# Beside a layer's last head: each output tile is projected as soon as its columns are transposed

## The chip, the cores and the metric

The kernel runs on one core of one Trainium2 chip. The metric is the device time of one execution in microseconds (us), lower is better. The kernel before takes 1910.28 us, the median of three runs that lie between 1908.68 and 1917.12 us. Five engines work side by side, each through its own instructions in order: PE (TensorE, matrix products and transposes), DVE (VectorE), ACT (ScalarE), POOL (GpSimd) and SP, which here only issues transfers. They wait for each other by semaphores.

## The reference, cut to what matters

Four layers run one after another over 640 tokens (128 of the prompt, 512 of the sample), that is five tiles of 128 tokens. A layer normalises x, projects it into eight heads, mixes the tokens within each head, and projects the mixed and gated heads back:

```python
for l in range(DEPTH):                       # 4 layers, kind = l % 3
    hs = rms_norm(xs, g_pre[l]) * (1.0 + sc_s) + sh_s
    if kind == 0:   ys = diff_attention(hs, da_w_in[j], da_w_out[j], ...)
    elif kind == 1: ys = retention(hs, ret_w_in[j], ret_w_out[j], ...)
    else:           ys = hgrn2(hs, hg_w_in[j], hg_w_out[j], ...)
    xs = xs + ga_s * rms_norm(ys, g_post[l])

# the end of each mixer, o is the mixed heads side by side
y = (o.reshape(B, T, HG_WIDTH) * jax.nn.silu(g)) @ w_out
```

Layers 0 and 3 are differential attention, layer 1 retention, layer 2 HGRN2. The change concerns the last line, `y @ w_out`, for the heads that are done while the last head is still being mixed.

## The kernel before

All products are in fp32 accuracy: a tensor is split into a high and a low part, and one product becomes three matmuls (high by high, high by low, low by high). For the output projection these are lines 458, 459 and 460 (`wide_unit`): one moving block of 512 columns each, over a column block k of 128 of the eight heads (16 in retention, whose heads are twice as wide). The text calls one such matmul a *product of w_out*.

Before a tile of y (128 tokens) can be projected, its columns must lie on the partitions. `y_to_h` transposes four blocks at a time on PE (line 448) into one PSUM bank; ACT copies the bank as the high part (`hh`, line 431) and DVE subtracts for the low part (`hl`, line 116). The bank is free after `hl`. PSUM is shared by two tags: "one", four buffers of one bank, and "two", two buffers of two banks.

PE's order is written out by hand; the other engines' order follows from a schedule that a list scheduler makes for that PE order. `weave(main, fill, span, room)` interleaves two generators: `main` mixes a head, `fill` projects the next head, and for every step of `main` as much of `fill` is issued as the ratio room/span allows. Beside the last head `fill` is `tail`: it transposes what is there of y (the six heads 0 to 5, in retention the eight column blocks 0 to 7, which lie in five buffers `ys` loaded from memory), takes four pieces of w_out, and then projects `hold` tiles into banks that it keeps open ("held"). `y_col` (line 497) then brings in the column of head 6 for all five tiles at once, and one product triple per held tile is added. When the last head is done `out_layer` finishes: the remaining tiles (2, 3 and 4 or only 4; tile 4 in a "two" buffer), the column of head 7, the second 512 columns and the norm.

Held tiles are 4 in layers 0 and 3, 2 in retention, 2 in HGRN2.

In HGRN2 the head's mix (`hg_mix`) runs over two directions. Each makes its decays on DVE, ACT and POOL, then transposes four blocks on PE (`pt`, line 1213), which ACT copies (`kt`), multiplies them by the values (`us`, line 1219), from which DVE makes the states `s` (line 1223) and ACT copies `so` (line 1226). Then both directions' scores (lines 1238 to 1242, into `fp`, a "two", and `gp`, a "one") are masked by DVE, and the head's output `o` (lines 1254 to 1257, a "two") is squared on ACT, scaled through `rs` on POOL, and written as y by DVE (line 637).

Of the kernel before, what the change touches and what calls it, by code (L numbers as in the profile page):

```python
# [21 lines left out]
P = 128  # L22
D = 1024
KT = 8
NS = 512
NP = 128
NT = 5
# [61 lines left out]
class Net:  # L89
# [374 lines left out]
    def tail(self, l, y, hold, st=None):  # L464

        self.mod_finish()
        two = KINDS[l] == 1
        self.held = {}
        ys = [y[:, tt, :] for tt in range(NT)]
        if two:  # L470
            for tt, (tag, bufs, dt) in enumerate((("sg", 2, F32), ("vh", 2, F32R), ("vl", 2, F32R), ("mraw", 2, F32), ("mraw", 2, F32))):
                if tag == "mraw":
                    ys[tt] = self.wp.tile([P, 4, 256], dt, tag=tag, bufs=bufs, name="ys")
                else:
                    ys[tt] = st.mp.tile([P, NT, 256], dt, tag=tag, bufs=bufs, name="ys")[:, 0:4, :]
                ys[tt] = ys[tt].rearrange("p a b -> p (a b)").bitcast(F32)
                self.nc.sync.dma_start(ys[tt], self.y_dram[:, tt, :])
        for tt in range(NT):
            yield from self.y_to_h(ys[tt], tt, KT if two else 6)
        self.ow = self.take(l, 0, 4)  # L480
        for tt in range(hold):
            ps = self.held[tt] = self.one()
            yield from self.wide_unit(ps, tt, self.ow, range(KT if two else 6), last=False)
        if not two:
            while hasattr(st, "done") and st.done < 6:
                yield None
            self.y_col(y, 6)
            yield 1.2
            for tt in range(hold):
                yield from self.wide_unit(self.held[tt], tt, self.ow, (6,), False, False)  # L490
# [559 lines left out]
    def hg(self, l, y):  # L1050
        nc, tc, t = self.nc, self.tc, self.t
        with tc.tile_pool(name=f"hg{l}", bufs=1, reuse_waits="tile") as mp:
            rs = self.const(mp, "rs")
            mf = mp.tile([P, NT, 64], U8, name="mf")
            mg = mp.tile([P, NT, 64], U8, name="mg")
            for m, n in ((mf, "mf"), (mg, "mg")):
                c = mp.tile([P, 640], F32, tag="w0", bufs=5, name="w0")[:, 0:320]
                nc.sync.dma_start(c, t["consts"][:, CWHERE[n][0]:sum(CWHERE[n])])
                nc.vector.tensor_copy(m.rearrange("p a b -> p (a b)"), c)
            ng = mp.tile([P, P], F32, name="ng")  # L1060
            nc.sync.dma_start(ng, t["hg_norm"][0].partition_broadcast(P))

            tt_ = nc.vector.tensor_tensor
            mx = mp.tile([P, 2, 8], F32, name="lmx")
            ex = mp.tile([P, 2, 4, 8], F32, name="lex")
            su = mp.tile([P, 2, 8], F32, name="lsu")
            tt_(out=mx, in0=self.lbl[:, :, 0, :], in1=self.lbl[:, :, 1, :], op=ALU.max)
            for i in (2, 3):
                tt_(out=mx, in0=mx, in1=self.lbl[:, :, i, :], op=ALU.max)
            tt_(out=ex, in0=self.lbl, in1=mx.unsqueeze(2).to_broadcast([P, 2, 4, 8]), op=ALU.subtract)  # L1070
            nc.scalar.activation(ex, ex, AF.Exp)
            tt_(out=su, in0=ex[:, :, 0, :], in1=ex[:, :, 1, :], op=ALU.add)
            for i in (2, 3):
                tt_(out=su, in0=su, in1=ex[:, :, i, :], op=ALU.add)
            nc.vector.reciprocal(su, su)
            tt_(out=ex, in0=ex, in1=su.unsqueeze(2).to_broadcast([P, 2, 4, 8]), op=ALU.mult)
            lb = mp.tile([P, 2, 8], F32, name="lb")
            tt_(out=lb, in0=ex[:, :, 0, :], in1=ex[:, :, 1, :], op=ALU.add)
            for i in range(2, l + 1):
                tt_(out=lb, in0=lb, in1=ex[:, :, i, :], op=ALU.add)  # L1080
            tt_(out=lb, in0=lb, in1=ex[:, :, 0, :], op=ALU.subtract)
            co = mp.tile([P, 3, 2, 8], F32, name="lco")
            for i, (a, b) in enumerate(((-0.5, 0.5), (0.5, 0.5), (0.5, -0.5))):
                nc.vector.tensor_scalar(out=co[:, i], in0=lb, scalar1=a, scalar2=b, op0=ALU.mult, op1=ALU.add)
            pz = [mp.tile([P, NT, 64], F32, name=f"z{d}") for d in range(2)]
            for z in pz:
                nc.vector.memset(z, 0.0)
            st = types.SimpleNamespace(mp=mp, l=l, rs=rs, mf=mf, mg=mg, ng=ng, co=co, pz=pz, iv={}, sg={}, h={})
            for _ in self.hg_proj(st, 0):
                pass  # L1090
            for h in range(HEADS):
                if h < 7:
                    self.weave(self.hg_mix(st, h, y), self.hg_proj(st, h + 1), 24.0, 30.0 if h < 6 else 18.0)
                else:
                    self.weave(self.hg_mix(st, h, y), self.tail(l, y, 2), 24.0, 12.0)

    def hg_proj(self, st, h):
        nc, t, mp = self.nc, self.t, st.mp
# [43 lines left out]
    def hg_mix(self, st, h, y):  # L1142
        nc, t, mp = self.nc, self.t, st.mp
        p, m = h // 2, h % 2
# [18 lines left out]
        for d in range(2):  # L1163
# [7 lines left out]
            if d == 0:  # L1171
                DV.tensor_tensor_scan(c, rs, g, 0.0, op0=ALU.mult, op1=ALU.add)
                ref, mid, last = 32, 63, 127
            else:
                DV.tensor_tensor_scan(c[:, ::-1], rs, g[:, ::-1], 0.0, op0=ALU.mult, op1=ALU.add)
                ref, mid, last = 31, 64, 0
# [30 lines left out]
            ke = tmp()  # L1207
            TT(PL, ke, k, ll, ALU.mult)
            yield 6.0
            pt = self.one([P, 4, P])  # L1210
            blocks = (0, 1, 2, 4) if d == 0 else (1, 2, 3, 4)
            for i, b in enumerate(blocks):
                nc.tensor.transpose(pt[:, i, :], bl(ke)[:, b, :], self.ident)
            kt = mp.tile([P, 4, P], F32, tag=f"kt{d}", name="kt")
            nc.scalar.activation(kt, pt, AF.Copy)
            yield 1.5
            us = self.one([P, 4, P])
            for i, b in enumerate(blocks):
                nc.tensor.matmul(us[:, i, :], kt[:, i, :], iv[:, b, ec], start=True, stop=True)
            order = (0, 1, 2) if d == 0 else (2, 1, 0)  # L1220
            for n, i in enumerate(order):
                b = blocks[i]
# [7 lines left out]
        (qf, kf, off, qef), (qb, kb, ofb, qeb) = res  # L1230
        fp = self.two()
        fd, fo = (fp[:, i, :320].rearrange("p (b i) -> p b i", i=64) for i in range(2))
        gp = self.one([P, NT, 64])
        mm = nc.tensor.matmul
        A, B = slice(0, 64), slice(64, 128)
        for b in range(NT):
# [196 lines left out]
```

## Time and profile before

| | |
|---|---|
| median of three runs | 1910.28 us (1908.68 to 1917.12) |
| profiled execution | 1908.83 us, span 1907.0 us |
| PE busy | 1814.8 us, 95% of the span |
| DVE / ACT / POOL busy | 1315.7 / 978.1 / 503.7 us |
| mean granted TensorE clock | 0.989 |

PE is busy for all but 92 us of the span. Busy time of a matmul is longer than its distance to the next one, since matmuls are pipelined; so the text takes distances from start to start. A granted clock of 1.00 is 2.4 GHz, 0.50 is 1.2 GHz. The last heads lie at about 380 to 405 us (layer 0), 905 to 975 (retention), 1400 to 1460 (HGRN2) and 1815 to 1845 (layer 3).

### The profile page before, as it was taken

Reading aid. Unit: us, or ns where it says so; the run is one execution under the profiler, and the core shown is the slowest. Engines: PE = TensorE matmul, PEld = TensorE weight load, DVE = VectorE, ACT = ScalarE, POOL = GpSimd, SP = SyncE. Lnnn points to the kernel's source line nnn. Section 1 sums busy time; section 2 is a strip of 40 time slices with the busy share of each in tenths; the row PEclk is TensorE's granted clock in tenths of the full one; section 3 lists DMA queues with packets and bytes.
Section 4 is the critical chain, followed back from the end, with each engine's and each line's share of the span. In section 5 each row is a group of like instructions: output and inputs, shape, how many; then the busy total and the mean of one; then the engine's idle time right before and its main releaser. Section 6 shows DMA issues by size and latency. Waiting matters only on the chain.

```text
span 1907.0 us, 32063 instructions
## 1 busy us (share of the span) xinstructions
PE 1814.8 (95%) x12060; PEld 1651.2 (87%) x12060; DVE 1315.7 (69%) x2553; ACT 978.1 (51%) x2271; POOL 503.7 (26%) x419
## 2 busy tenths in 40 slices
PE   6989999999999999999999999999979989999998
PEld 4888999977888888888878899999978879999976
DVE  5768788857788998774334667676764766667754
ACT  3456666555444344433343456666654545655552
POOL 0414343202222222222101323342431521222101
PEclk9999999999999999999999999999989999999999
DMA  9644445414345445433323222222214463443322
GB/s 323 177 114 133 133 138 144 128 57 155 126 133 168 140 143 157 142 124 101 104 99 111 85 70 73 64 62 73 62 42 138 132 172 89 112 115 88 107 72 101
DMA packets 231963, 224.59 MB, mean 118 GB/s; under 512 B 11664, under 2 KB 201984, under 8 KB 231808
## 3 DMA queue, kind: packets, MB, share of 16 engines
q1 hardware_dynamic: 231344, 222.16, 38.7%
q8 instruction: 95, 1.56, 0.4%
q14 instruction: 60, 0.49, 0.1%
q10 hardware_dynamic: 464, 0.39, 0.1%
HBM read 174.79 MB, written 18.35 MB: 101 GB/s over the span
## 4 chain that ended last, share of the span: by engine, by line
PE 57%; DVE 20%; ACT 8%; DMA 5%; issue 4%; POOL 3%; SPq 2%; DVEq 0%; ACTq 0%; POOLq 0%
PE one L458 7%; PE one L460 7%; PE one L459 7%; PE one L250 4%; PE one L251 4%; PE one L252 4%; DVE macc L361 4%; DVE wlo L116 3%; PE one L821 3%; PE one L225 3%; PE one L226 2%; PE one L227 2%; ACT whi L178 2%; DMA kz<-ks 1%; DVE nm L785 1%
## 5 line engine op out<-in xcount | busy, mean ns | idle before, releaser
L250 PE MATMUL one<-hh,whi 128*128 128x320 f32 x1152 | 365.4, 317 | 9.3 <-ACT qp L760 6.4
L251 PE MATMUL one<-hl,whi 128*128 128x320 f32 x1152 | 357.0, 310 | 0.0
L252 PE MATMUL one<-hh,wlo 128*128 128x320 f32 x1152 | 356.8, 310 | 0.0
L116 DVE TENSOR_TENSOR wlo<-raw,whi 128x1024 fp32r<-128x1024 f32 x192 | 246.4, 1290 | 134.2 <-ACT whi L178 132.9
L458 PE MATMUL one<-whi,hh 128*128 128x512 f32 x744 | 303.0, 407 | 5.8 <-ACT yo L554 2.5
L460 PE MATMUL one<-whi,hl 128*128 128x512 f32 x744 | 296.1, 398 | 1.0 <-DVE hl L116 0.5
L459 PE MATMUL one<-wlo,hh 128*128 128x512 f32 x744 | 295.6, 397 | 0.0
L178 ACT ACTIVATE whi<-raw 128x1024 fp32r<-128x1024 f32 x192 | 201.3, 1056 | 138.4 <-PE one L251 52.0
L250 PEld LDWEIGHTS one<-hh,whi 128*128 128x128 f32 x1152 | 217.6, 189 | 12.0 <-ACT qp L760 6.8
L361 DVE SCALAR_TENSOR_TENSOR macc<-mraw,smod,macc 128x256 f32<-128x256 f32 x432 | 216.3, 544 | 10.2 <-POOL macc L363 9.6
L251 PEld LDWEIGHTS one<-hl,whi 128*128 128x128 f32 x1152 | 217.6, 189 | 0.5
L252 PEld LDWEIGHTS one<-hh,wlo 128*128 128x128 f32 x1152 | 217.3, 189 | 0.3 <-DVE wlo L116 0.3
L225 PE MATMUL one<-whi,hh 128*128 128x256 f32 x720 | 207.8, 289 | 0.0
L226 PE MATMUL one<-wlo,hh 128*128 128x256 f32 x720 | 201.1, 279 | 0.0
L227 PE MATMUL one<-whi,hl 128*128 128x256 f32 x720 | 201.1, 279 | 0.0
L458 PEld LDWEIGHTS one<-whi,hh 128*128 128x128 f32 x744 | 141.3, 190 | 38.5 <-DVE p L1007 4.0
L460 PEld LDWEIGHTS one<-whi,hl 128*128 128x128 f32 x744 | 140.8, 189 | 37.1 <-DVE hl L116 2.3
L459 PEld LDWEIGHTS one<-wlo,hh 128*128 128x128 f32 x744 | 141.3, 190 | 29.4
L363 POOL TENSOR_TENSOR macc<-macc,mpart 128x512 f32<-128x512 f32 x64 | 94.7, 1481 | 180.9 <-ACT macc L359 65.3
L391 POOL TENSOR_TENSOR rs<-ms,mhalf 128x1 f32<-128x1 f32 (+1 forms) x72 | 66.0, 917 | 288.3 <-DVE ms L384 152.9
L225 PEld LDWEIGHTS one<-whi,hh 128*128 128x128 f32 x720 | 135.5, 188 | 1.5
L226 PEld LDWEIGHTS one<-wlo,hh 128*128 128x128 f32 x720 | 135.6, 188 | 0.0
(344 smaller groups left out, 3765.0 us busy)
## 6 DMA issues: line engine op xcount, KB each, us to landing
mraw<-in_w_mod SPq DMA_DIRECT2D x96, 512.0 KB, 4.2
raw<-in_da_w_in SPq DMA_DIRECT2D x56, 512.0 KB, 4.2
raw<-in_hg_w_in SPq DMA_DIRECT2D x36, 512.0 KB, 3.8
raw<-in_ret_w_in SPq DMA_DIRECT2D x64, 256.0 KB, 3.1
kk<-ks SPq DMA_DIRECT2D x64, 160.0 KB, 3.4
kz<-ks SPq DMA_DIRECT2D x64, 160.0 KB, 3.2
qq<-q SPq DMA_DIRECT2D x64, 128.0 KB, 3.5
raw<-in_da_w_out SPq DMA_DIRECT2D x16, 512.0 KB, 3.5
```

The lines of the kernel that those rows point to most:

```text
L116: return (eng or self.nc.gpsimd).tensor_tensor(out=out, in0=full, in1=hi.bitcast(F32), op=ALU.subtract)
L178: self.nc.scalar.activation(hi, raw, AF.Copy)
L225: mm(out, xh, wh[:, k % 4, :], start=(first and k == ks[0]), stop=False)
L226: mm(out, xh, wl[:, k % 4, :], start=False, stop=False)
L227: mm(out, xl, wh[:, k % 4, :], start=False, stop=(last and k == ks[-1]))
L250: nc.tensor.matmul(ps, wh[:, k, :], self.hh[:, k, c], start=(k == 0), stop=False)
L251: nc.tensor.matmul(ps, wh[:, k, :], self.hl[:, k, c], start=False, stop=False)
L252: nc.tensor.matmul(ps, wl[:, k, :], self.hh[:, k, c], start=False, stop=(k == KT - 1))
L361: nc.vector.scalar_tensor_tensor(out=m, in0=raw[:, k, :], scalar=c, in1=m, op0=ALU.mult, op1=ALU.add)
L458: mm(ps, xh, wh, start=(first and k == ks[0]), stop=False)
L459: mm(ps, xh, wl, start=False, stop=False)
L460: mm(ps, xl, wh, start=False, stop=(last and k == ks[-1]))
```

## The change

`tail` takes its w_out pieces first, transposes tiles 0 and 1, projects tile 0, transposes tiles 2 and 3, projects tile 1, transposes tile 4, and projects what is left of the held tiles. It does so in all four layers. HGRN2's last head holds four tiles instead of two, with a room of 22 instead of 12 in the interleaving, and its `pt`, `us` and `gp` use the "two" buffers. The number of PE matmuls is the same.

```diff
-        for tt in range(NT):
-            yield from self.y_to_h(ys[tt], tt, KT if two else 6)
+        n = KT if two else 6
         self.ow = self.take(l, 0, 4)
-        for tt in range(hold):
-            ps = self.held[tt] = self.one()
-            yield from self.wide_unit(ps, tt, self.ow, range(KT if two else 6), last=False)
+        for tt in range(2):
+            yield from self.y_to_h(ys[tt], tt, n)
+        for tt in range(max(hold, 3)):
+            if tt < hold:
+                ps = self.held[tt] = self.one()
+                yield from self.wide_unit(ps, tt, self.ow, range(n), last=False)
+            for i in ((2, 3), (4,), ())[min(tt, 2)]:
+                yield from self.y_to_h(ys[i], i, n)
...
-                    self.weave(self.hg_mix(st, h, y), self.tail(l, y, 2), 24.0, 12.0)
+                    self.weave(self.hg_mix(st, h, y), self.tail(l, y, 4), 24.0, 22.0)
...
-            pt = self.one([P, 4, P])
+            bank = self.one if h < 7 else lambda shape: self.two([P, 2 * shape[1], P])[:, 0:shape[1], :]
+            pt = bank([P, 4, P])
...
-            us = self.one([P, 4, P])
+            us = bank([P, 4, P])
...
-        gp = self.one([P, NT, 64])
+        gp = self.one([P, NT, 64]) if h < 7 else self.two()[:, 0, :320].rearrange("p (b i) -> p b i", i=64)
```

Lines after line 478 carry numbers that are 4 (from `hg_mix`'s `pt` on, 5) higher in the kernel with the change: line 785 becomes 789, 863 becomes 867, 1223 becomes 1228.

How it moves instructions is shown at three places. The first is DVE in layer 0 beside the last head, before: `hl` are the low parts of the transposed columns, `nm` (line 785) the maxima of the last head's scores, `rc` and `pe` (lines 861 to 863) the combination of its two softmaxes.

```order
L863 SCALAR_TENSOR_TENSOR pep<-pep,rc 128x128
L116 TENSOR_TENSOR hl<-one,hh 128x4x128
L116 TENSOR_TENSOR hl<-one,hh 128x2x128
L116 TENSOR_TENSOR hl<-one,hh 128x4x128
L116 TENSOR_TENSOR hl<-one,hh 128x2x128
L785 TENSOR_REDUCE nm<-two 128x1 x2
L861 RECIPROCAL rc<-sums 128x1
L862 SCALAR_TENSOR_TENSOR rc<-sums,nlam,rc 128x1
L863 SCALAR_TENSOR_TENSOR pe<-pe,rc 128x640
```

The same place on DVE with the change:

```order
L867 SCALAR_TENSOR_TENSOR pep<-pep,rc 128x128
L789 TENSOR_REDUCE nm<-two 128x1 x2
L865 RECIPROCAL rc<-sums 128x1
L866 SCALAR_TENSOR_TENSOR rc<-sums,nlam,rc 128x1
L867 SCALAR_TENSOR_TENSOR pe<-pe,rc 128x640
L116 TENSOR_TENSOR hl<-one,hh 128x4x128
L116 TENSOR_TENSOR hl<-one,hh 128x2x128
L116 TENSOR_TENSOR hl<-one,hh 128x4x128
L116 TENSOR_TENSOR hl<-one,hh 128x2x128
```

The low parts of tiles 2 and 3 moved behind the four steps of the head's first query tile. Layer 3 has the same order.

The second place is DVE in HGRN2 beside the last head, before: `c`, `w`, `qd`, `of`, `qe` and `dl` are the second direction's decays and scaled queries and keys, between which `hl` of y's tiles stand.

```order
L1175 SCALAR_TENSOR_TENSOR c_15106<-c_rs,w_15104 128x640
L116 TENSOR_TENSOR hl<-one,hh 128x2x128
L1150 TENSOR_TENSOR w_15108<-c_15106 128x640
L116 TENSOR_TENSOR hl<-one,hh 128x4x128
L116 TENSOR_TENSOR hl<-one,hh 128x2x128
L1150 TENSOR_TENSOR w_15118<-c_15106 128x640
L116 TENSOR_TENSOR hl<-one,hh 128x4x128
L1150 TENSOR_TENSOR qd_15114<-q,w_15110 128x640
L116 TENSOR_TENSOR hl<-one,hh 128x2x128
L116 TENSOR_TENSOR hl<-one,hh 128x4x128
L1150 TENSOR_TENSOR of_15123<-k_15102,w_15120 128x5x64
```

The same place on DVE with the change:

```order
L1179 SCALAR_TENSOR_TENSOR c_15113<-c_rs,w_15111 128x640
L116 TENSOR_TENSOR hl<-one,hh 128x2x128
L1154 TENSOR_TENSOR w_15115<-c_15113 128x640
L1154 TENSOR_TENSOR w_15125<-c_15113 128x640
L1154 TENSOR_TENSOR qd_15121<-q,w_15117 128x640
L1154 TENSOR_TENSOR of_15130<-k_15109,w_15127 128x5x64
L1154 TENSOR_TENSOR of_15130<-q,w_15127 128x5x64
L1154 TENSOR_TENSOR qe_15135<-q,w_15133 128x512
L1207 COPY dl_15137<-w_15133 128x5
L116 TENSOR_TENSOR hl<-one,hh 128x4x128
L116 TENSOR_TENSOR hl<-one,hh 128x2x128
```

The low parts of tiles 2 and 3 moved behind the whole of the second direction.

The third place is PE in HGRN2 where head 6's column is brought in (line 497, with the change 501) before the head's output `o`, before:

```order
L460 MATMUL one<-whi,hl 128x512
L497 MATMUL two<-c_ident,y 128x128 x5
L1254 MATMUL two<-iv,w_15214 128x128
L1256 MATMUL two<-s_14979,qe_15008 128x128
L1257 MATMUL two<-s_14979,qe_15128 128x128
```

The same place on PE with the change:

```order
L460 MATMUL one<-whi,hl 128x512
L501 MATMUL two<-c_ident,y 128x128 x5
L458 MATMUL one<-whi,hh 128x512
L459 MATMUL one<-wlo,hh 128x512
L460 MATMUL one<-whi,hl 128x512
L1259 MATMUL two<-iv,w_15252 128x128
L1261 MATMUL two<-s_14979,qe_15008 128x128
```

The products of head 6's column for tile 0 now stand between the column's transposes and the head's output.

On SP two things move: in retention the two loads of `mraw` (modulation weights of the next layer) stand behind the store of the new state, and in HGRN2 two loads of the next layer's weights change places with a store of x.

## Rows read from the trace of the kernel before

**Rows 1.** The page: busy time of each engine, and the chain that ended last.
```profile
PE 1814.8 (95%) x12060; PEld 1651.2 (87%) x12060; DVE 1315.7 (69%) x2553; ACT 978.1 (51%) x2271; POOL 503.7 (26%) x419
...
PE 57%; DVE 20%; ACT 8%; DMA 5%; issue 4%; POOL 3%; SPq 2%; DVEq 0%; ACTq 0%; POOLq 0%
```

**Rows 2.** Windows in HGRN2: busy time of PE, PEld, DVE, ACT, POOL; granted clock.
```profile
1410.00:1420.00 10.00, 8.12 (x30) 6.25 (x29) 9.74 (x16) 7.71 (x14) 4.17 (x3) 0.50 0.09 33
1420.00:1430.00 10.00, 10.00 (x99) 8.70 (x99) 2.85 (x8) 1.15 (x3) 0.81 (x1) 0.87 0.05 13
```

**Rows 3.** Timeline of PE, HGRN2's last head: start, length, instruction, [idle before].
```profile
1405.26 0.45 PE L448 MATMUL one<-c_ident,y 128*128 128x128 f32 x2 [2.63 <-ACT th L1138]
1409.20 2.39 PE L448 MATMUL one<-c_ident,y 128*128 128x128 f32 x10 [3.49 <-DVE hl L116]
...
1416.56 0.79 PE L458 MATMUL one<-whi,hh 128*128 128x512 f32 x1 [0.99 <-ACT kt L1215]
...
1422.67 0.39 PE L459 MATMUL one<-wlo,hh 128*128 128x512 f32 x1
...
1432.13 0.71 PE L497 MATMUL two<-c_ident,y 128*128 128x128 f32 x5
1432.68 0.39 PE L1254 MATMUL two<-iv,w 128*128 128x128 f32 x2
...
1437.77 0.48 PE L458 MATMUL one<-whi,hh 128*128 128x512 f32 x1
...
1451.85 0.71 PE L497 MATMUL two<-c_ident,y 128*128 128x128 f32 x5
```

**Rows 4.** Window on DVE's line 1150 (second direction in HGRN2): busy time, clock.
```profile
1411.70:1419.40 7.70, 5.38 (x6) 0.50 0.00 0
```

**Rows 5.** Timeline of DVE, HGRN2's last head.
```profile
1414.11 0.68 DVE L116 TENSOR_TENSOR hl<-one,hh 128x512 fp32r<-128x512 f32 x1
...
1427.45 1.11 DVE L1223 SCALAR_TENSOR_TENSOR s<-s,dl,one 128x128 f32<-128x128 f32 x3 [5.10 <-PE one L1219]
...
1433.61 0.82 DVE L116 TENSOR_TENSOR hl<-two,hh 128x640 fp32r<-128x640 f32 x1 [3.45 <-ACT hh L498]
...
1439.30 1.39 DVE L637 SCALAR_TENSOR_TENSOR y<-two,rs,sg 128x128 f32<-128x128 f32 x5 [1.35 <-POOL rs L391]
```

**Rows 6.** Timeline of ACT, HGRN2's last head.
```profile
1411.63 0.60 ACT L431 ACTIVATE hh<-one 128x512 fp32r<-128x512 f32 x1 [0.41 <-PE one L448]
...
1428.65 0.28 ACT L1226 ACTIVATE so<-one 128x128 f32<-128x128 f32 x1 [2.88 <-DVE s L1223]
...
1432.88 0.70 ACT L498 ACTIVATE hh<-two 128x640 fp32r<-128x640 f32 x1 [1.75 <-PE two L497]
```

**Rows 7.** Timeline of PE, retention's last head and the second column pass.
```profile
936.59 0.39 PE L458 MATMUL one<-whi,hh 128*128 128x512 f32 x1
...
939.38 0.40 PE L458 MATMUL one<-whi,hh 128*128 128x512 f32 x1
...
964.40 0.50 PE L458 MATMUL one<-whi,hh 128*128 128x512 f32 x1 [2.45 <-ACT yo L554]
```

**Rows 8.** Timeline of DVE, retention: the last tile of the last head's y.
```profile
942.41 0.48 DVE L637 SCALAR_TENSOR_TENSOR y<-one,rs,sg 128x256 f32<-128x256 f32 x1
```

**Rows 9.** Windows after idle stretches of PE, in retention and at layer 3's start.
```profile
966.00:968.00 2.00, 2.00 (x6) 1.60 (x5) 1.23 (x1) 0.27 (x1) 0.00 (x0) 0.50 0.68 262
...
1534.00:1538.00 4.00, 0.98 (x6) 0.98 (x7) 3.37 (x8) 2.47 (x6) 1.36 (x2) 1.00 0.80 212
```

**Rows 10.** Timeline of PE, layer 3: the last head's first scores and what follows.
```profile
1826.37 0.30 PE L783 MATMUL two<-kk,qq 128*128 128x320 f32 x1
...
1827.54 0.40 PE L458 MATMUL one<-whi,hh 128*128 128x512 f32 x1
1827.78 0.39 PE L459 MATMUL one<-wlo,hh 128*128 128x512 f32 x1
```

**Rows 11.** Timeline of DVE, layer 3: the last step on those scores.
```profile
1830.15 0.89 DVE L863 SCALAR_TENSOR_TENSOR pe<-pe,rc 128x640 f32<-128x640 f32 x1
```

## The prediction

> **What bounds the kernel now.** I read the page first, then the windows of the four last heads, then PE's timeline there, and last DVE's and ACT's. PE is busy 95% of the span and holds 57% of the chain that ended last [rows 1]. So an instruction that is only moved on PE costs nothing; the change can gain where PE waits or runs at half clock beside a last head, and lose where it makes a new wait there. The place to gain is HGRN2. Between 1410 and 1420 PE is busy 8.12 of 10 us at a granted clock of 0.50, which is the 1.2 GHz level, and between 1420 and 1430 the clock is 0.87 in the mean [rows 2]. The timeline shows why: PE waits for `hl`, transposes, waits again, and only at 1416.56 come products of w_out; from 1422.67 on they run at full clock [rows 3]. The other three layers have no such stretch beside their last heads.
>
> **HGRN2.** The work from 1409.20 to the column of head 7 at 1451.85 takes 42.65 us [rows 3], and the change has the same instructions in it, only in another order. From 1422.67 on it is dense at full clock: 29.18 us. The 13.47 us before hold 1.88 us of idle PE (10.00 less 8.12, [rows 2]); the other 11.6 run at half clock and would take 5.8. So the whole needs 35.0 us at full clock without a wait. What it takes with the change is 35.0 plus the half clock left plus the new waits.
>
> Half clock. The twelve transposes of tiles 0 and 1, the last two at 1405.26 [rows 3], are done before 1409.20, so tile 0's products begin there and are dense. In the kernel before, dense work from 1416.56 had the full clock by 1422.67, 6.1 us later; the same again costs 3.05 us. Bounds: 0 and 5.8, all of what it costs now. I take 3.0.
>
> Waits. Each edit that adds one, with its price:
> - Tiles 2 and 3. Tile 0's bank is held, so the second chunk of tile 3 needs the bank of tile 2's first chunk, whose `hl` now stands on DVE behind the second direction. Those six steps take 5.38 us [rows 4]. From 1411.7 they end at about 1417.2, `hl` at 0.68 more [rows 5], so at 1418 or a little later; behind this `hl` on DVE wait only the next ones. PE has 18 products (at half clock about 7.7 us, by twice the 0.24 of [rows 10]) and some transposes from 1409.20 on, and comes between 1416 and 1418. I take 0.9 us; bounds 0 and 2.3.
> - Tile 2's products open a bank right behind tile 4's transposes, and need `hh` and `hl` of the chunk in it: 0.60 [rows 6] and 0.68 [rows 5], of which I take 1.2 us. Bounds 0 and 1.3.
> - `gp` in a "two" buffer has to wait until `us` is read: three `s` from 1427.45 and then `so`, which ends at 1428.93 [rows 5, 6]: 1.5 us. The old `gp` lay in a free bank and waited for nothing. Behind it stand the scores, the mask and everything of the head. Bounds 0.5 and 1.6.
> - Head 6's column: its transposes at 1432.13, `hl` ends at 1434.43 [rows 3, 5]. Now 0.55 us of transposes and then the head's output hide this, since `o` stands next on PE at 1432.68. With the change tile 0's products stand there: two can go once `hh` is there at 1433.58 [rows 6], the third needs `hl`. 2.30 less 0.55 and less two products of 0.24 [rows 10] is 1.3 us. Behind it `o` and the whole of head 7 are late by as much. Bounds 0.9 and 1.7.
> - Tile 4 is now held off by the "two" buffer of `o`, until DVE has written y: from 1432.68 to 1440.69 is 8.0 us [rows 3, 5]. The kernel before had 42 products of tiles 2 and 3 to run meanwhile; now these are done earlier. What stands between is `o`, six products and the gates (1432.68 to 1437.77, 5.1 us, [rows 3]) and three more products, 0.7 us: a wait of 2.2 us. Bounds 1.5 and 3.
>
> Sum: 35.0 + 3.0 + 0.9 + 1.2 + 1.5 + 1.3 + 2.2 = 45.1 against 42.65: **+2.5 us**.
>
> **Retention.** The early products come before the transposes that wait now, but the held bank brings waits for `hl` before the head's output; I estimate from `hh` and `hl` (0.60 and 0.68) that half of one, 0.6 us, is left. What counts comes behind it. Tile 2 needs the one-bank buffer in which the last part of the output lies, until y is written from it at 942.89 [rows 8]. From the end of the output at 936.59 [rows 7] that is 6.3 us. The kernel before has twelve products there and tile 2 in another bank at 939.38, 2.8 us after; with the change tile 2 starts 3.5 later, with the 0.6 4.1. Tile 4's transposes lie in that gap. Some of it comes back: at 964.40 PE waits 2.45 us for ACT to empty a bank [rows 7], and behind that it runs at half clock (0.50 from 966 to 968, at least 1.0 us, [rows 9]). Both shrink if PE comes later. If all comes back 0.65 is left, if nothing, 4.1; I take the middle, **+2.1 us**. The two `mraw` loads that move on SP wait for tile 4's last transposes, and the loads of x and of w_out queue behind them; x waits for y anyway, so I price that at nothing; without that cover it would come on top of the 4.1.
>
> **Layers 0 and 3.** Here the early transposes keep their waits, and the four held tiles stay four. In layer 3 the first scores start at 1826.37 = S, the combination on DVE ends at 1831.04 = S + 4.7 [rows 10, 11]. `hl` of tile 2's first chunk now stands behind it and ends at S + 5.35 (0.68, [rows 5]). PE has eight scores (1.17 us), six products (1.4, [rows 10]) and eleven transposes (each about 0.12, half of a tenth of the 2.39 at half clock of [rows 3]; 1.2) and is at tile 3's second chunk at S + 3.7. The wait is 1.65 us, and 0.25 for tile 1's bank: **+1.9 us in each**. Bounds: −0.8 (if some of the early waits go too) and 2.8. PE is dense behind it, so nothing gives it back.
>
> **Sum.** 1.9 + 2.1 + 2.5 + 1.9 = 8.4 us on the profiled 1908.83 is 1917.2. That execution is 1.45 us under the median and 0.15 above the fastest run, two of three lie near it, so I keep it as the base: **1917 us**.
>
> **The rule on the clock.** Behind the 2.45 us gap in retention PE fell to half clock, and a gap in which PE was busy 0.98 of 4 us left it at 1.00 [rows 9]. The Trainium skill, TensorE: Matmul & The Clock Gate, section "Why this matters for your kernels", asks that PE have no longer idle gaps between bursts of matmuls, since the array then goes back to half rate. By it new waits would cost more than their length; these two rows agree and disagree. It is the second rival.
>
> **Rivals.**
> - *The gain is what is left.* Dense products bring the clock back at once in HGRN2 (−5.8), and DVE and ACT reach their steps earlier, since the transposes' copies no longer crowd between the head's own, so that of the waits priced above only the smaller half remains (+3). Retention is at +0.65, less some of the early waits 0; layers 0 and 3 at −0.8 each: −4.5 in all, 1904; at the best, with no wait left, 1900. For it: half clock and waits of 1410 to 1420. Against: every wait priced has its releaser behind more work on DVE or ACT. Chance 0.17.
> - *The new gaps drop the clock.* Places: tile 4 in HGRN2 (2.2 us) and tile 2 in retention (over 2 us). Price: a drop costs between 1.0 (window 966 to 968) and 3.0 us (1416.56 to 1422.67, half of 6.1). It decides once a gap is as long as the 2.45 us that did it before. With two drops of 2 us the time is 1921, with a further one in layers 0 or 3, 1923: slower beyond 0.5%. Chance 0.23.
> - *Nothing net.* The waits fall on work that another wait hid, half of them each; the half clock saved pays the rest: 1910. For it: PE waits in these places before and after. Chance 0.20.
>
> **How the numbers follow.** My forecast, 1912 to 1921, has 0.40. About 0.5% (9.5 us) is what a measurement of this kernel can tell from no change, so faster lies under 1900.7 and slower above 1919.8 on the median 1910.28. Faster takes half of the first rival, 0.09. Slower takes nine tenths of the second, 0.21, and a quarter of the forecast, 0.10: 0.31. The rest is 0.60. The range goes from 1903 to 1924; it leaves out the best of the first rival, the worst of the second, and waits at all upper bounds (1928).
>
> **What would show it.** In PE's timeline: products of w_out in HGRN2 by 1410 and full clock by 1416; a wait in front of `gp` (line 1245) on ACT, one in front of the products behind line 501, one of about 2 us before tile 4 on DVE's y; in retention tile 2 at 943 to 944, and a shorter wait before the second column pass; in layers 0 and 3 a wait of 1 to 2 us on `hl` 3 to 4 us behind the first scores. The prediction is wrong if head 7's column in HGRN2 comes before 1451 counted from the same start, or if tile 2 in retention starts as early as before.

## The result and the profile after

The kernel with the change takes 1924.48 us (median of 7, 1920.17 to 1931.67), the kernel before 1911.04 us in its 7 runs beside it: ratio 1.0069, interval 1.005 to 1.0088. It is slower by about 13 us, beyond the 0.5% that can be told from no change, and half a microsecond above the range that was forecast. The profiled execution took 1924.37 us, its span is 1922.6 us.

The page of the kernel with the change, busy time and the chain that ended last; [rows 1] are those of before:

```profile
PE 1816.8 (94%) x12060; PEld 1652.9 (86%) x12060; DVE 1316.4 (68%) x2553; ACT 978.1 (51%) x2271; POOL 502.1 (26%) x419
...
PE 57%; DVE 20%; ACT 8%; DMA 5%; issue 4%; POOL 3%; SPq 2%; DVEq 0%; POOLq 0%; ACTq 0%
```

PE is busy for 2 us more in a span that is 15.6 us longer: nearly all of the time went into PE standing still.

PE's timeline beside HGRN2's last head with the change (start, length, instruction, idle before and its releaser), from the first transposes to the column of head 7, to be read against [rows 3]:

```profile
1410.41 1.25 PE L448 MATMUL one<-c_ident,y 128*128 128x128 f32 x10
...
1418.23 0.79 PE L458 MATMUL one<-whi,hh 128*128 128x512 f32 x1 [3.50 <-DVE hl L116]
...
1427.06 0.44 PE L448 MATMUL one<-c_ident,y 128*128 128x128 f32 x2 [0.32 <-DVE hl L116]
...
1434.78 0.50 PE L458 MATMUL one<-whi,hh 128*128 128x512 f32 x1 [1.19 <-DVE hl L116]
...
1442.13 0.34 PE L1245 MATMUL two<-qd,kd 128*64 128x64 f32 x4 [1.30 <-ACT so L1231]
...
1449.70 0.50 PE L458 MATMUL one<-whi,hh 128*128 128x512 f32 x1 [0.79 <-ACT hh L502]
...
1458.96 0.50 PE L458 MATMUL two<-whi,hh 128*128 128x512 f32 x1 [2.03 <-DVE y L641]
...
1463.27 0.71 PE L501 MATMUL two<-c_ident,y 128*128 128x128 f32 x5
```

The five new waits stand where the prediction had put them: tile 3's transposes, tile 2's bank, `gp`, head 6's column, tile 4. The windows of the same stretch (busy time of PE, PEld, DVE, ACT, POOL, granted clock), against [rows 2]:

```profile
1414.00:1424.00 10.00, 6.20 (x16) 4.76 (x17) 9.13 (x16) 7.63 (x14) 2.95 (x3) 0.66 0.16 53
1424.00:1430.00 6.00, 5.62 (x37) 4.58 (x36) 4.26 (x8) 3.27 (x7) 3.40 (x3) 1.00 0.01 3
```

Full clock is back by 1424, 13.6 us after the first transposes; before it took 21.

Layer 0 with the change, PE's timeline behind the first scores, then DVE's:

```profile
400.22 0.44 PE L448 MATMUL one<-c_ident,y 128*128 128x128 f32 x2 [1.21 <-DVE hl L116]
...
408.13 1.38 PE L825 MATMUL two<-v,at 128*128 128x128 f32 x10 [0.42 <-ACT at L818]
```

```profile
398.68 0.89 DVE L867 SCALAR_TENSOR_TENSOR pe<-pe,rc 128x640 f32<-128x640 f32 x1
399.48 2.06 DVE L116 TENSOR_TENSOR hl<-one,hh 128x512 fp32r<-128x512 f32 x4
```

`hl` starts when the combination of the softmaxes ends, and PE waits for it. Layer 3 has the same two waits. They make 1.63 of the 2.2 us by which the stretch is longer in each of the two layers (table below); the rest was not found.

Retention with the change, PE's timeline, against [rows 7]:

```profile
931.02 0.65 PE L448 MATMUL one<-c_ident,ys 128*128 128x128 f32 x4 [1.08 <-DVE hl L116]
...
946.07 0.66 PE L448 MATMUL one<-c_ident,ys 128*128 128x128 f32 x4 [1.97 <-DVE hl L116]
948.55 0.48 PE L458 MATMUL one<-whi,hh 128*128 128x512 f32 x1 [1.82 <-DVE y L641]
...
973.42 0.50 PE L458 MATMUL one<-whi,hh 128*128 128x512 f32 x1 [0.69 <-ACT yo L558]
```

The wait of 2.45 us before the second column pass shrank to 0.69. The half clock that stood behind it [rows 9] did not go, it moved ahead, behind the new waits, and in the second profile of this kernel it lasts longer there (0.50 from 947 to 953). A window of the kernel with the change there:

```profile
950.00:954.00 4.00, 4.00 (x13) 3.10 (x13) 1.27 (x2) 0.00 (x0) 0.00 (x0) 0.66 0.92 326
```

The four stretches in all profiles that bear on it, in us from start to start on PE (layers 0 and 3: first transposes to head 6's column; retention: first transposes to the transposes of y in the second pass; HGRN2: first transposes to head 7's column). The kernels below the second line are those of the next section.

| profile | layer 0 | retention | HGRN2 | layer 3 |
|---|---|---|---|---|
| before, three profiles | 35.4, 35.4, 35.4 | 64.4, 63.9, 64.3 | 50.5, 50.4, 49.9 | 35.4, 35.3, 35.4 |
| whole change, two | 37.5, 37.6 | 67.0, 68.2 | 52.9, 56.4 | 37.6, 37.6 |
| layers 0 and 3 only | 37.6 | 62.7 | 47.9 | 37.6 |
| layers 0, 3 and retention | 37.5 | 67.8 | 47.7 | 37.6 |
| retention only | 35.4 | 66.7 | 50.3 | 35.4 |
| HGRN2 only | 35.3 | 64.0 | 57.2 | 35.4 |

The means of the first two lines differ by 2.2, 3.4, 4.4 and 2.2 us, 12.2 together; the medians of the times differ by 13.4 in the first comparison and 12.9 in the second one below.

### The profile page after: what moved, and what is told of

It is laid out like the page before. It is cut to its first block, busy times and chain, and to the rows that moved or that the text cites. A ratio compares the mean times of both kernels' runs of the same rounds, so it can differ in the third digit from the quotient of the medians.

```text
span 1922.6 us, 32065 instructions
## 1 busy us (share of the span) xinstructions
PE 1816.8 (94%) x12060; PEld 1652.9 (86%) x12060; DVE 1316.4 (68%) x2553; ACT 978.1 (51%) x2271; POOL 502.1 (26%) x419
## 4 chain that ended last, share of the span: by engine, by line
PE 57%; DVE 20%; ACT 8%; DMA 5%; issue 4%; POOL 3%; SPq 2%; DVEq 0%; POOLq 0%; ACTq 0%
PE one L458 7%; PE one L460 7%; PE one L459 7%; PE one L250 4%; PE one L251 4%; PE one L252 4%; DVE macc L361 4%; DVE wlo L116 3%; PE one L225 3%; PE one L825 3%; PE one L226 3%; PE one L227 3%; ACT whi L178 1%; DVE nm L789 1%; PE two L787 1%
## 5 line engine op out<-in xcount | busy, mean ns | idle before, releaser
L178 ACT ACTIVATE whi<-raw 128x1024 fp32r<-128x1024 f32 x192 | 201.3, 1055 | 137.6 <-PE one L251 49.9
L363 POOL TENSOR_TENSOR macc<-macc,mpart 128x512 f32<-128x512 f32 x64 | 94.3, 1475 | 185.5 <-ACT macc L359 66.7
```

The costliest lines, as they stand in the source:

```text
L178: self.nc.scalar.activation(hi, raw, AF.Copy)
```

## The experiments

**HGRN2 only.** The change in layer 2, the old order in the others.

```diff
+        if KINDS[l] in (2,):
             ... the new tail
+        else:
+            ... the old tail
```

> The change in HGRN2 alone; layers 0, 1 and 3 transpose all tiles first as before. Theory A (the loss is the sum of the waits that the profile of the changed kernel names beside the four last heads: 1.3 net in layer 0, 2.9 in retention, 2.4 in HGRN2, 2.2 in layer 3, some 9 us, and what is beyond is the spread between executions): +2.4 us in HGRN2's last head, with waits of 0.3, 1.2, 1.3, 1.2 and 2.0 us in the same places; total about +3 us on the median of before (1911), 1914, ratio 1.001 to 1.003. Theory B (the change makes PE fall to half clock more often elsewhere, so each part costs more than its waits): +5 us or more, 1916, with drops to 0.50 in the profile that before does not have.

Measured: ratio 1.0021 (1.0011 to 1.0031), median 1916.36 against 1910.88. The interval holds the totals of both theories. Inside the head it is not what A said: 57.2 us, and a second drop to 0.50, which B had named. PE's timeline of this kernel:

```profile
1409.85 0.80 PE L458 MATMUL one<-whi,hh 128*128 128x512 f32 x1 [3.24 <-DVE hl L116]
...
1420.73 0.69 PE L448 MATMUL one<-c_ident,y 128*128 128x128 f32 x2 [3.57 <-DVE hl L116]
...
1459.20 0.71 PE L509 MATMUL two<-c_ident,y 128*128 128x128 f32 x5
```

and its windows:

```profile
1406.00:1412.00 6.00, 2.76 (x7) 1.97 (x8) 5.89 (x11) 4.87 (x7) 1.59 (x2) 0.50 0.28 87
1412.00:1418.00 6.00, 5.16 (x28) 4.15 (x27) 5.62 (x8) 4.20 (x8) 3.03 (x2) 0.93 0.00 1
1418.00:1424.00 6.00, 3.27 (x10) 2.65 (x10) 4.03 (x7) 1.59 (x4) 1.53 (x1) 0.63 0.01 3
1424.00:1428.00 4.00, 4.00 (x17) 3.52 (x17) 1.04 (x3) 0.28 (x1) 0.00 (x0) 0.70 0.00 0
```

Here PE stood 3.57 us for `hl` before tile 3's last transposes, in place of 0.32, and behind this wait the clock fell a second time. Two things made the wait longer. Full clock came back sooner, so PE was ready 15.1 us after the first transposes (at 1402.03), and 16.3 us after them in the first profile of the whole change: that is 1.2 us. And the first `hl` of tile 2 began on DVE 18.0 us after them in place of 15.9: that is 2.1 us. DVE is level in the two profiles up to 14.5 us; then two of its instructions before `hl` took longer, beside POOL (rows in the last section). So 1.2 us of what the clock gave back PE waited for on DVE; the larger part is DVE being late.

**Layers 0, 3 and retention.** The new order there, HGRN2 as before (`KINDS[l] in (0, 1)`).

> The new order of transposes and products in layers 0, 1 and 3 alone; HGRN2 as before. Theory A: +1.3 in layer 0 net, +2.9 in retention, +2.2 in layer 3, together +6.4: 1917, ratio 1.003 to 1.004; waits of 1.2 and 0.4 us in layers 0 and 3, of 1.1, 2.0 and 1.8 us in retention, and HGRN2 as before (50.5 us from its first transposes to the column of head 7). Theory B: +9 us or more, 1920.

Measured: 1.0020 (1.0008 to 1.0032), 1915.44. The waits in the three heads are as expected (1.21 and 0.42; 1.07, 1.97 and 1.82), the stretches too. The total is 1.8 us under the expected +6.4, and HGRN2 is not as before: 47.7 us in place of 50.2, although nothing in it was edited.

**Four held, old order.** In all layers the old order of transposes; HGRN2 holds four tiles with room 22 and the double banks.

```diff
-        ... the new tail
+        ... the old tail
             self.weave(self.hg_mix(st, h, y), self.tail(l, y, 4), 24.0, 22.0)
```

> HGRN2's last head holds four tiles and uses the double banks, but all tiles are transposed first as before, in all layers. Theory A: the waits in front of gp (1.3), head 6's column (about 1.2 with its third product) and tile 4 (2.0) belong to holding four and to the double banks, not to the order: they stay, and half clock until about 1422 stays too; the waits for hl among the transposes stay as in before. From the first transposes to head 7's column 50.5 + 4.5 = 55 us; total about 1915. Rival (the order makes the waits): these three waits are gone, 50 to 51 us, 1911.

Measured: 1.0014 (1.0001 to 1.0027), 1915.40; HGRN2 53.0 us. PE's timeline of this kernel:

```profile
1436.82 0.34 PE L1241 MATMUL two<-qd,kd 128*64 128x64 f32 x4 [1.30 <-ACT so L1227]
...
1444.39 0.50 PE L458 MATMUL one<-whi,hh 128*128 128x512 f32 x1 [0.79 <-ACT hh L498]
...
1453.64 0.50 PE L458 MATMUL two<-whi,hh 128*128 128x512 f32 x1 [2.03 <-DVE y L637]
```

The three waits are the same to a hundredth: they belong to holding four tiles and to the double banks, not to the order. The expected 55 us was too high by 2: the wait of 0.99 us for `kt` at 1416.56 [rows 3] is gone with the double banks, the products start 13.5 us after the first transposes in place of 15.2, and full clock is back after 16.5 us in place of 21.

**New order, two held.** HGRN2 alone; two tiles, room 12 and one-bank buffers as before.

```diff
-    self.weave(self.hg_mix(st, h, y), self.tail(l, y, 4), 24.0, 22.0)
+    self.weave(self.hg_mix(st, h, y), self.tail(l, y, 2), 24.0, 12.0)
```

> HGRN2 alone gets the new order of transposes and products, but holds two tiles, with room 12 and one-bank buffers as before; other layers as before. Theory A: the early products bring full clock some 5 us earlier (3 us of gain), and gp, head 6's column and tile 4 don't wait; 1 to 2 us of waits for hl before tile 1's products stay. From the first transposes to head 7's column 48 to 49.5 us against 50.5, total 1908 to 1910, hardly to be told from before. Rival (the order itself costs, by hl behind the second direction on DVE): 51 us or more.

Measured: 0.9988 (0.9977 to 0.9998), median 1908.79 against 1910.88; HGRN2 48.7 us. PE's timeline and two windows of this kernel:

```profile
1409.81 0.80 PE L458 MATMUL one<-whi,hh 128*128 128x512 f32 x1 [3.51 <-DVE hl L116]
...
1421.30 0.44 PE L448 MATMUL one<-c_ident,y 128*128 128x128 f32 x2 [0.55 <-DVE hl L116]
...
1450.69 0.71 PE L509 MATMUL two<-c_ident,y 128*128 128x128 f32 x5
```

```profile
1406.00:1416.00 10.00, 6.26 (x18) 4.52 (x18) 9.55 (x16) 7.62 (x13) 2.94 (x3) 0.66 0.15 53
1416.00:1426.00 10.00, 7.88 (x60) 6.29 (x62) 6.00 (x12) 3.85 (x9) 3.21 (x3) 1.00 0.03 8
```

Products start 7.8 us after the first transposes in place of 15.2, full clock is back by 1416, and none of the waits at `gp`, head 6's column and tile 4 is there, as theory A said. This is the fastest version, 2 us under before, with an interval that ends just under 1.

Order and holding can now be told apart. With two tiles held the new order gives 0.9988. With four held it gives 1.0021 and the old order 1.0014, which the intervals do not separate. So HGRN2's loss comes with holding four tiles (room and double banks were changed along with it), and not with the new order.

**The whole change again.** The same kernel, timed beside 29 more runs of before.

> The kernel with the whole change, unaltered, timed again beside more runs of before. The two halves measured alone gave ratios of 1.0021 and 1.0020. Theory A (the parts add up, and the first 1.0069 lies in the spread): 1.0041, 1918 to 1920. Theory B (the parts act on each other: what one part delays moves the next stretch into half clock): 1.006 to 1.007, 1923 to 1925.

Measured: 1.0070 (1.0058 to 1.0082), 1924.14 against 1911.19. Theory B's number: the two halves fall short of the whole by 0.3%. The next kernel shows a reason other than B's. The second profile has 56.4 us in HGRN2. PE's timeline of this second profile, then its windows behind these two waits (DVE's rows for the first wait are in the last section):

```profile
1427.39 0.45 PE L448 MATMUL one<-c_ident,y 128*128 128x128 f32 x2 [2.19 <-DVE hl L116]
...
1460.65 0.51 PE L458 MATMUL two<-whi,hh 128*128 128x512 f32 x1 [2.02 <-DVE y L641]
```

```profile
1428.00:1431.00 3.00, 3.00 (x9) 2.43 (x10) 0.69 (x2) 0.26 (x1) 0.51 (x1) 0.50 0.02 5
1461.00:1465.00 4.00, 4.00 (x13) 3.08 (x12) 2.08 (x2) 0.64 (x1) 0.00 (x0) 0.60 0.45 150
```

Both waits cost the clock in this execution. In the first profile neither did (1.00 from 1424 on). From tile 4's first product to head 7's column this profile takes 5.84 us and the first 4.31, so this fall of the clock cost 1.5 us. Before tile 3 PE was ready 15.2 us after the first transposes (at 1410.04) in place of 16.3, and `hl` began 16.6 us after them in place of 15.9.

**Layers 0 and 3 only** (`KINDS[l] in (0,)`, HGRN2 as before).

> The new order of transposes and products in layers 0 and 3 alone, everything else as before. Theory A: the waits of 1.2 us on hl and 0.4 us on at in both layers, 35.4 us becoming 37.5 from the first transposes to head 6's column in each, less what layer 0 gives back before layer 1: +3.5 us, ratio 1.0018, and so retention nearly nothing in the time of the two together (1.0020). Rival (retention is the dearer, as its waits of 1.1, 2.0 and 1.8 us against the 2.45 us that they take the place of say): +1.5 us, 1.0008.

Measured: 1.0003 (0.9993 to 1.0012), 1912.13. The two stretches are 2.2 us longer each, as expected, and yet the total hardly moves. HGRN2 takes 47.9 us in place of 50.2. The order of the instructions says why: the list scheduler put other instructions first beside HGRN2's last head, on DVE and ACT (presumably since the edit of layer 0 shifted the times that it reckons with; no run shows that). DVE there, before (left) and in this kernel (right), in order:

```
c                       c
hl 128x256              hl 128x256
w                       hl 128x512
hl 128x512              hl 128x256
hl 128x256              w
w                       hl 128x512
hl 128x512              hl 128x256
qd                      w
hl 128x256              qd
hl 128x512              hl 128x512
of                      hl 128x256
```

PE's timeline and a window of this kernel:

```profile
1409.67 1.71 PE L448 MATMUL one<-c_ident,y 128*128 128x128 f32 x6 [0.25 <-DVE hl L116]
...
1412.31 0.78 PE L458 MATMUL one<-whi,hh 128*128 128x512 f32 x1
```

```profile
1413.00:1423.00 10.00, 8.70 (x58) 6.82 (x58) 7.15 (x11) 4.55 (x10) 4.77 (x3) 0.98 0.03 8
```

The low parts come earlier, the waits of 0.64 and 0.99 us before the first product are gone, that product starts 13.1 us after the first transposes in place of 15.2, and full clock is back within a microsecond or two. The kernel with layers 0, 3 and retention has the same order and 47.7 us; retention alone has the order of before and 50.3. So both kernels in which layer 0 was edited contain a gain of some 2.4 us in a part that was not edited, and the whole change, which rewrites that part, does not have it. Of the 5 to 6 us by which the two halves fall short of the whole that covers 2.4; the rest is inside the intervals taken together. The three parts measured alone (layers 0 and 3 1.0003, HGRN2 1.0021, retention 1.0027 below) give 1.0051, with 2.4 us more 1.0064, which lies in both intervals of the whole change. Parts that act on each other through the clock are not needed to explain the whole. One caution: this profile is the fastest of the kernel's 12 runs, and in its retention no half clock follows the wait before the second column pass (2.35 us), so its 62.7 us there are luck.

**Three held.** HGRN2 alone, `tail(l, y, 3)` with room 17.

> HGRN2 alone gets the change, but holds three tiles with room 17 in place of four with 22; other layers as before. Theory A (each wait is a question of what stands between releaser and waiter): tile 3's 21 products stand before tile 4 again, so the 2.0 us in front of tile 4 go, and the 1.3 us in front of gp and those at head 6's column stay; 2 us less than with four tiles, ratio about 1.001, 1912 to 1914. Rival (the waits for hl at tile 3 and the half clock decide, and not how many tiles are held): as with four, 1.002, 1915 to 1916.

Measured: 0.9999 (0.9991 to 1.0008), 1911.04; HGRN2 51.4. The wait before tile 4 is gone, those at `gp` (1.30) and head 6's column (0.79) stayed, as theory A said; the total is a microsecond or two below its number.

**Two held, one copy per tile.** The six columns of a tile in one double buffer, one `hh` and one `hl` of 768 columns (`y_to_h(ys[tt], tt, n, 8)`).

> HGRN2 alone: new order, two tiles held, and the six columns of a tile transposed into one double buffer, so that they are copied by one hh and one hl of 768 columns in place of two. Others as before. The one-bank buffers are then free for the held tiles, pt and us. Theory A: the waits for one bank beside tiles 2 and 3 (0.3, 0.6 and 0.7 us with two one-bank copies) shrink, while the first products wait as long or 0.3 us longer, since hl of 768 columns is later than that of 512: 0 to 1.5 us under the new order with two tiles, 1907 to 1909. Rival (DVE's order sets when the products may start, not the banks): 1909 to 1911, as with two one-bank copies or worse.

Measured: 0.9995 (0.9984 to 1.0005), 1910.27; HGRN2 48.7, the same as with two copies, and the rival's number. The waits for one bank are gone, but PE now waits 2.22 us for `kt` (0.78 with two copies) and 1.44 us for `hl` behind head 6's column, so this run does not show what the banks alone cost.

**DVE relieved.** The whole change, and four steps of HGRN2's last second direction on POOL.

```diff
+            VP = PL if h == 7 and d == 1 else DV
-            TT(DV, qd, q, e1, ALU.mult)
+            TT(VP, qd, q, e1, ALU.mult)
             ... the same for both halves of `of` and for `qe`
```

> The whole change, and beside HGRN2's last head four steps of the second direction (qd, both halves of of, qe) run on POOL in place of DVE, so that hl of tiles 2 and 3 no longer stands behind them; PE's order is the same instruction by instruction. Theory A (this DVE order makes PE wait before tile 3's last two transposes, 0.3, 2.2 and 3.6 us in three profiles, the longer the sooner full clock came back, and after the long waits PE falls to half clock a second time): the wait is under 0.5 us, no second stretch at half clock within 20 us of the first, and from the first transposes to head 7's column 51 to 53 us in place of 52.9, 56.4 and 57.2; total 2 to 4 us under the whole change, 1920 to 1922, ratio 1.005. Rival (the waits in front of gp, head 6's column and tile 4 make the second drop, or POOL becomes late): 55 us or more and 1924.

Measured: 1.0061 (1.0049 to 1.0073), 1922.02; HGRN2 53.8. PE's timeline and a window of this kernel:

```profile
1422.23 0.44 PE L448 MATMUL one<-c_ident,y 128*128 128x128 f32 x2 [0.32 <-DVE hl L116]
...
1454.73 0.50 PE L458 MATMUL two<-whi,hh 128*128 128x512 f32 x1 [2.03 <-DVE y L641]
```

```profile
1455.00:1459.00 4.00, 4.00 (x12) 3.10 (x12) 2.15 (x2) 0.70 (x1) 0.00 (x0) 0.57 0.58 206
```

The long wait at tile 3 is not there (0.32 us, and 0.68 more before the next products), nor the drop behind it. PE was ready 15.1 us after the first transposes (at 1406.77), as early as in the two profiles with long waits. So an early full clock alone does not make the long wait; what stands before `hl` on DVE has to add to it. Tile 4's wait cost the clock here, again 1.5 us (5.84 us from its product to head 7's column), without which the 53.8 us would lie in the expected 51 to 53. The time in the total, 1 to 2 us less, is not clear of the whole change's interval.

**Retention only** (`KINDS[l] in (1,)`).

> The new order in retention alone; everything else as before. Theory A (waits of 1.1, 2.0 and 1.8 us against the small ones and part of the 2.45 us they take the place of): 67 to 68 us from the first transposes to the second column pass's gates against 64.4, total +3.4 us, 1914.5, ratio 1.0018. Rival (layers 0 and 3 cost more in the time than alone, retention little): +1.5 us or less, 1.0008.

Measured: 1.0027 (1.0017 to 1.0036), 1915.54; the stretch 66.7 us, 2.5 more than before's mean of 64.2. The total is 2 to 3 us more than the stretch, with an interval that begins less than 1 us above it; where these lie was not found.

**Before, profiled twice more.**

> The kernel before, unaltered, profiled once more. Theory A (the stretch at half clock beside HGRN2's last head differs from one execution to the next, and the first profile had a long one): from the first transposes to head 7's column 47.5 to 48.5 us, as in the two other kernels that have the old HGRN2 (47.7 and 47.9), and full clock back some 5 us sooner than in the first profile. Rival (50.5 us is the kernel's own time there): 50 to 51.

> The same once more. Theory A: 47.5 to 48.5 us, or 50 to 51 in the minority. Rival: 50 to 51 again.

Measured: 50.4 and 49.9 us in HGRN2. The rival is right: 50.5 is the kernel's own time there, and the base of the prediction's HGRN2 sum was sound.

## Why the prediction was wrong

The direction and the places were right: the change is slower, by waits beside the last heads, in all four layers. The time came out 7 us higher than the forecast, and the likeliest outcome that was named, no change that can be told (0.60), did not come.

- *Layers 0 and 3, +1.9 each:* measured 2.2 each. The wait on `hl` was 1.21 in place of 1.65 plus 0.25, and one of 0.42 for `at` was not foreseen; some 0.6 us of the 2.2 was not found.
- *Retention, +2.1:* measured 3.4 (2.5 to 4). The waits are as said. The step that failed is what comes back: I took the middle between "all" and "nothing" of the 2.45 us and of the half clock behind it. Of the wait 1.76 us came back, of the half clock nothing: in all five profiles with the new order it stands behind the new waits of 1.97 and 1.82 us. By the granted clock of the windows (an estimate) it costs 1.7 us in each of before's three profiles and in three of these five, and 3.4 in the other two.
- *HGRN2, +2.5:* in the first profile 52.9 against 50.5, which is +2.4, and the terms one by one, forecast and measured: tile 3 0.9 and 0.32, tile 2's bank 1.2 and 1.19, `gp` 1.5 and 1.30, head 6's column 1.3 and 0.79 (0.3 more before its third product), tile 4 2.2 and 2.03. That the sum came out is in part luck, since that profile was the mild one: the second has 56.4, HGRN2 only 57.2, and the mean of the whole change's two is 4.4 above before's. The step that failed is "I take 0.9 us; bounds 0 and 2.3" for tiles 2 and 3, with the half clock as a separate term. Tile 3's wait measured 0.32, 2.19 and 3.57 us, the last above its bound. In the two long ones PE came 1.2 us sooner with its early full clock, and `hl` came 0.7 and 2.1 us later, as DVE instructions before it took longer beside POOL, which the fixed 5.38 us of [rows 4] could not say. Behind both the clock then fell again. What holding four tiles costs is in the terms for `gp`, head 6's column and tile 4, and these were sized well.
- *The second rival* (new gaps drop the clock, chance 0.23) is what happened beside the waits, in some executions: at tile 3 in two profiles of three, at tile 4 in two of five, and in retention in all, where before has it too. Its condition, a gap as long as 2.45 us, did not hold: tile 4's waits of 2.02 to 2.04 us were followed by 0.50 in those two profiles and by 1.00 in the other three, and a wait of 3.24 us at 1537 in the kernel before [rows 9] by 1.00. In the prediction this rival excluded the forecast; in the runs both hold at once, and the forecast should have carried part of its price.
- *The base:* the profiled 1908.83 is near the low end of before; the median of the 7 runs is 2.2 us higher. Keeping the single execution as base cost these 2.2.
- *Sums in the working:* the middle of 0.65 and 4.1 in retention is 2.4 and not 2.1, and 18 products at twice 0.24 are 8.6 us and not 7.7 (the trace's 0.43 between products at half clock, 1417.15 to 1417.58, gives 7.7). The 1928 for all upper bounds stands on the median; on the base 1908.83 it is 1926.6.

2.2 for the base, 1.3 for retention, 1.9 for HGRN2 and 0.6 for layers 0 and 3 are 6.0 of the 7 us; the rest is inside the interval of the ratio. The first rival's gain came nowhere in the whole change: its full clock was there, and waits took it back. With two tiles held it came in part.

## What to carry to other kernels

When early work is moved ahead on the engine that is the bound, look at which engine in order releases what comes next: part of the time won arrives there as a wait, and a wait in front of dense matmuls can cost the clock as well. Price clock and wait together, not as two terms, and give the fall of the clock a chance and not a threshold. Test the parts of a change by themselves: here the reordering with two tiles held cost nothing, and holding more tiles did. Where a scheduler sets the other engines' order, an edit in one layer can reorder another; compare the orders of untouched parts before adding up parts that were measured apart.

## What the runs showed of the hardware

A DVE instruction can take a microsecond longer while POOL works. In the kernel with HGRN2 only, DVE's timeline, then POOL's:

```profile
1416.49 1.53 DVE L1162 TENSOR_TENSOR of<-q,w 128x320 f32<-128x320 f32 x1
1417.95 0.68 DVE L1162 TENSOR_TENSOR qe<-q,w 128x512 f32<-128x512 f32 x1
1418.56 1.53 DVE L1215 COPY dl<-w 128x5 f32<-128x5 f32 x1
1420.00 1.61 DVE L116 TENSOR_TENSOR hl<-one,hh 128x512 fp32r<-128x512 f32 x3
```

```profile
1416.18 1.50 POOL L1162 TENSOR_TENSOR w<-c 128x640 f32<-128x640 f32 x1
1418.53 1.53 POOL L1162 TENSOR_TENSOR w<-k,w 128x640 f32<-128x640 f32 x1 [0.85 <-ACT w L1218]
```

In the first profile of the whole change the same two DVE instructions meet no POOL work:

```profile
1424.87 0.48 DVE L1154 TENSOR_TENSOR of<-q,w 128x320 f32<-128x320 f32 x1
1425.27 0.68 DVE L1154 TENSOR_TENSOR qe<-q,w 128x512 f32<-128x512 f32 x1
1425.87 0.16 DVE L1207 COPY dl<-w 128x5 f32<-128x5 f32 x1
1426.31 1.95 DVE L116 TENSOR_TENSOR hl<-one,hh 128x512 fp32r<-128x512 f32 x3 [0.28 <-ACT hh L431]
```

In the second profile of the same kernel `qe` meets POOL, DVE's rows and then POOL's:

```profile
1424.93 1.73 DVE L1154 TENSOR_TENSOR qe<-q,w 128x512 f32<-128x512 f32 x1
...
1426.66 1.61 DVE L116 TENSOR_TENSOR hl<-one,hh 128x512 fp32r<-128x512 f32 x3
```

```profile
1424.68 1.43 POOL L1154 TENSOR_TENSOR w<-c 128x640 f32<-128x640 f32 x1 [0.43 <-POOL kd L1154]
```

A copy of five columns takes 0.16 us alone and 1.53 beside a POOL instruction of 1.53 that starts with it; the product of 320 columns 0.48 and 1.53; that of 512 columns 0.68 and 1.73. In HGRN2 only these are 2.4 us more on DVE, of which 2.1 arrive at `hl` (18.0 us after the first transposes against 15.9, where `hl` had waited 0.28 us for ACT); in the second profile of the whole change `hl` begins 0.7 us later. Which instructions meet differs between two executions of one kernel. The Trainium skill, SBUF — State Buffer, section "Who interferes with whom", says that DVE and GpSimd share a pair of ports, that an instruction of one can block the other's for its whole length, and that a DVE instruction with two inputs in SBUF or one in a two-port mode is subject to it; these rows agree, though none shows in which mode the copy ran.
